# Output projection of a hybrid attention layer: eight products of quarters against Strassen's seven, and two ways to spread a row of scales

## The chip, the cores and the metric

One core of a Trainium2 chip. The metric is the device time in microseconds (us) of one execution; the kernel before has a median of 1061.15 us over three runs (1060.97 to 1061.85). The core has a matrix engine (TensorE, PE in the rows), VectorE (DVE), ScalarE (ACT), GpSimd (POOL) and the queue engine SP, which issues most DMAs. Each works through its own queue in order, and semaphores tie the queues together.

## The reference

One decoder layer in float32, 512 tokens, width 2048. The part that the change touches is the output projection and the norm behind it:

```
y = jnp.einsum('btm,md->btd', jnp.concatenate([o_a, o_b], axis=-1), w_out[l])
x = x + rmsnorm(y, norm_post_g[l])
```

`o_a` (8 heads x 128, differential attention) and `o_b` (8 heads x 128, sparse attention over latent keys) are each multiplied by a SiLU gate. The einsum is a product of 512x2048 and 2048x2048.

## The kernel before, in words

The kernel keeps activations transposed, as tiles of 128 features x 512 tokens. Precision comes from splitting: each float32 operand x becomes a high part (ScalarE's cast to float32r) and a low part (VectorE's x minus high), and a product is three matmuls, high x high, high x low and low x high.

**Weights.** `unit` (L55) lists every weight tile in the order of use. `load_to` (L90) loads a unit by a DMA on SP into one of two `wf` buffers, `split_to` (L104) splits it on ScalarE and VectorE (L124, L125) into one of three `wh` and three `wl` buffers, and `use` (L129) hands it to the matmuls and asks for the loads and splits of the units up to three or four ahead. Loads and splits get a priority up to 600 places earlier (`lead`, L86). The program is written in one order, and a scheduler that follows priorities and its own timeline sets the final order of each engine's queue.

**Spread.** `rstd` (L194) makes four columns of scales by a power on GpSimd. `spread` (L198) turns them into a row on all 128 partitions: GpSimd multiplies the identity by each column (L202, four times), and a matmul with a tile of ones sums it over the partitions (L203). It is called three times at the start (L217, L286, L306) and once in each head of group A (`head_a`, L524).

**Heads.** Eight heads of group A, then eight of group B (L585 on). `head_b` (L527) computes scores, softmax, transposes (L424) and values (L435); its transposed probabilities lie in tiles named pt0a, pt0b to pt3a, pt3b, and its result, times the gate, goes to `go[8 + h]` (L554). In head 7, before `head_b`, the finished gate tiles 0 to 14 are split (L590), and tile 15 at L593.

**Output projection (L598 to L669).** Four column blocks n of 512 columns. For n < 3, eight weight units (two contraction tiles each) are used in turn, and each serves four token blocks i: `part` (L605) issues 2 x 3 matmuls of 512 columns (L609 to L611). `done` (L613) squares a finished bank with its sum on ScalarE and multiplies it by the broadcast norm gain on VectorE (L617, one input in PSUM, one in SBUF). The last block, n = 3, keeps its eight units and goes token block by token block (L651 to L653), the last one in two halves of 256 columns, so that the residual (L633), the power (L661), the final scaling and addition (L668, L666) and the store (L669) of one block lie under the matmuls of the next.

Of the kernel before, what the change touches and what calls it, by code (L numbers as in the profile page):

```python
# [25 lines left out]
def hybrid_layer(tc, xT, xn, wck, wT, wik, wva, wuv, wo, gpre, gpost, sub, kvg, ikg, lq1, lk1, lq2, lk2, relb, oneh, out):  # L26
    nc = tc.nc
    from contextlib import ExitStack
    with ExitStack() as st:
# [50 lines left out]
        for n in range(4):  # L80
            for kp in range(8):
                unit(wo[n, kp], (2, 512))
        stage, ready, flags = {}, {}, {"begin": None}
# [5 lines left out]

        def load_to(n):  # L90
            while pos["load"] < min(n, len(units)):
# [4 lines left out]
                t = S.tile([128, 1024], F32, name=nm, bufs=bf)  # L96
                with tc.high_priority(lead()):
                    nc.sync.dma_start(t[:, :c], ap)
                stage[i] = t
                pos["load"] += 1  # L100

        last = [("qk", 4)] * 4 + [("v", 3)] * 3 + [("ck0", 1), ("ck1", 1)] + [("wh", 3), ("wl", 3)] * 3 + [("pt0a", 1)]

        def split_to(n):  # L104
            while pos["split"] < min(n, len(units)):
                i = pos["split"]
                load_to(i + 1)
                c = units[i][1][0] * units[i][1][1]
                t = stage.pop(i)
                names = [("wh", 3), ("wl", 3)]  # L110
                if i >= len(units) - 8:
                    names = [last.pop(0), last.pop(0)]
                w = []
                for nm, bf in names:
                    if nm == "pt0a":
                        w.append([S.tile([128, 512], F32R, name=x, bufs=1) for x in ("pt0a", "pt0b")])
                    else:
                        a = S.tile([128, 1024], F32R, name=nm, bufs=bf)
                        w.append([a[:, :512], a[:, 512:]] if units[i][1][1] == 512 else [a[:, :c]])
                m = c // len(w[0])  # L120
                with tc.high_priority(lead()):
                    for q in range(len(w[0])):
                        src = t[:, q * m:(q + 1) * m]
                        nc.scalar.copy(w[0][q], src)  # L124
                        nc.vector.tensor_tensor(w[1][q], src, w[0][q].bitcast(F32), op=OP.subtract)  # L125
                ready[i] = w
                pos["split"] += 1

        def use(ahead=3):  # L129
            i = pos["use"]  # L130
            pos["use"] += 1
            if ahead:
                load_to(i + ahead + 1)
                split_to(i + ahead)
            nk, n = units[i][1]
            w = ready.pop(i)
            per = nk // len(w[0])
            return [[w[a][k // per][:, (k % per) * n:(k % per + 1) * n] for k in range(nk)] for a in range(2)]
# [13 lines left out]
        ones = S.tile([128, 128], F32, name="ones")  # L152
        nc.gpsimd.memset(ones, 1.0)
# [422 lines left out]
        oh_, ol_ = [], []  # L576

        def split_o(m):
            a = S.tile([128, 512], F32R, name=f"hh{m}")
            b = S.tile([128, 512], F32R, name=f"hl{m}")  # L580
            split((a, b), go[m])
            oh_.append(a)
            ol_.append(b)

        for h in range(8):  # L585
# [3 lines left out]
            if h == 7:  # L589
                for m in range(15):  # L590
                    split_o(m)
# [6 lines left out]
        for n in range(4):  # L598
            gB = S.tile([128, 512], F32, name="strip", bufs=2)
            nc.gpsimd.dma_start(gB, bcast(gpost[n], 512))  # L600
            if n % 2 == 0:
                banks = [proj_bank(), proj_bank(), proj_bank(), lg_bank()]
            else:
                banks = [lg_bank(), tr_bank(), tr_bank(), av_bank()]
            def part(kp, i, wh, wl):  # L605
                ts = slice(i * 128, (i + 1) * 128)
                for k in range(2):
                    kk = 2 * kp + k
                    nc.tensor.matmul(banks[i], oh_[kk][:, ts], wh[k], start=(kk == 0), stop=False)  # L609
                    nc.tensor.matmul(banks[i], oh_[kk][:, ts], wl[k], start=False, stop=False)  # L610
                    nc.tensor.matmul(banks[i], ol_[kk][:, ts], wh[k], start=False, stop=(kk == 15))  # L611

            def done(i):  # L613
                junk = S.tile([128, 512], F32, name="a3")
                nc.scalar.activation(junk, banks[i], AF.Square, accum_out=ssy[:, i, n:n + 1])
                y = S.tile([128, 512], F32, name=f"go{i * 4 + n}")
                nc.vector.tensor_tensor(y, banks[i], gB, op=OP.mult)  # L617
                ys[i, n] = y

            if n < 3:  # L620
                for kp in range(8):
                    wh, wl = use()
                    for i in range(4):
                        part(kp, i, wh, wl)
                for i in range(4):
                    done(i)
                continue
            ws = []
            for i in range(4):
                xs = []  # L630
                for q in range(4):
                    xr = S.tile([128, 512], F32, name="e" if q < 2 else "tq", bufs=2)
                    nc.sync.dma_start(xr, xn[i * 128:(i + 1) * 128, q * 512:(q + 1) * 512])  # L633
                    xs.append(xr)
                y = S.tile([128, 512], F32, name=f"go{i * 4 + n}")
                ys[i, n] = y
                base = S.tile([128, 1], F32, name="base", bufs=2)
                nc.vector.tensor_reduce(base, ssy[:, i, :3], axis=mybir.AxisListType.X, op=OP.add)
                nc.vector.tensor_scalar(base, base, 1.0 / D, EPS, op0=OP.mult, op1=OP.add)
                ry = S.tile([128, 1], F32, name="ry", bufs=2)  # L640
                cuts = (0, 512) if i < 3 else (0, 256, 512)
                for a, b in zip(cuts, cuts[1:]):
                    o = (banks[i] if a == 0 else proj_bank())[:, a:b]
                    for kp in range(8):
                        if i == 0:
                            ws.append(use())
                        wh, wl = ws[kp]
                        for k in range(2):
                            kk = 2 * kp + k
                            ts = slice(i * 128, (i + 1) * 128)  # L650
                            nc.tensor.matmul(o, oh_[kk][:, ts], wh[k][:, a:b], start=(kk == 0), stop=False)  # L651
                            nc.tensor.matmul(o, oh_[kk][:, ts], wl[k][:, a:b], start=False, stop=False)
                            nc.tensor.matmul(o, ol_[kk][:, ts], wh[k][:, a:b], start=False,  # L653
                                             stop=(kk == 15))
                    junk = S.tile([128, 512], F32, name="a3")
                    sl = ssy[:, i, 3:4]
                    nc.scalar.activation(junk[:, :b - a], o, AF.Square, accum_out=sl)
                    nc.vector.scalar_tensor_tensor(ry if b == 512 else base, sl, 1.0 / D, base,
                                                   op0=OP.mult, op1=OP.add)
                    nc.vector.tensor_tensor(y[:, a:b], o, gB[:, a:b], op=OP.mult)  # L660
                nc.gpsimd.tensor_tensor(ry, ry, mhalf[:, 0:1], op=OP.pow)  # L661
                for q in range(4):
                    if i == 3 and q == 1:
                        t = S.tile([128, 512], F32, name="sq", bufs=1)
                        nc.scalar.activation(t, ys[i, q], AF.Copy, scale=ry)
                        nc.gpsimd.tensor_tensor(ys[i, q], t, xs[q], op=OP.add)  # L666
                    else:
                        nc.vector.scalar_tensor_tensor(ys[i, q], ys[i, q], ry, xs[q], op0=OP.mult, op1=OP.add)  # L668
                    nc.sync.dma_start(out[i * 128:(i + 1) * 128, q * 512:(q + 1) * 512], ys[i, q])  # L669
# [11 lines left out]
def _layout(inputs):  # L681
# [21 lines left out]
    wo = np.stack([tiles(f["w_out"].reshape(D, D)[:, 512 * n:512 * n + 512], 2) for n in range(4)])  # L703
# [33 lines left out]
```

## Time and profile before

| what | value |
|---|---|
| median of three runs | 1061.15 us |
| profiled execution, its own time | 1062.16 us |
| span of the profiled execution | 1060.1 us |
| TensorE busy | 1048.4 us (99%), 5403 matmuls |
| VectorE busy | 568.0 us (54%) |
| ScalarE busy | 420.9 us (40%) |
| GpSimd busy | 69.5 us (7%) |
| mean granted clock | 0.997 |

Times inside an execution count from the start of the span. The span ends with the last store; the profiled execution's own time is about 2 us longer than its span. A busy TensorE is not TensorE at its peak, since matmuls are pipelined and overlap in the rows.

### The profile page before, as it was taken

To read this page: it belongs to the slowest core of one execution; us is meant where nothing else is said; L and a number is where in the kernel's file an instruction comes from. 1 tells how busy PE (TensorE), PEld (TensorE's weight loads), DVE (VectorE), ACT (ScalarE), POOL (GpSimd) and SP (SyncE) were. 2 spreads that over 40 slices of the span, in tenths; PEclk is the share of its full clock that TensorE was granted. 3 is DMA by queue.
4 is the path that set the end of the run, shared out by engine and by line. 5 is a ranking of instruction groups with operands and counts; after the bars stand their busy time and mean duration, and the time that the engine had idled before them with its cause. 6 is when DMAs were issued, how large, how long until landed. Compare 5 with 4: busy or idle time off the path is not lost.

```text
span 1060.1 us, 13936 instructions
## 1 busy us (share of the span) xinstructions
PE 1048.4 (99%) x5403; PEld 898.0 (85%) x5403; DVE 568.0 (54%) x1144; ACT 420.9 (40%) x789; POOL 69.5 (7%) x102
## 2 busy tenths in 40 slices
PE   8999999999999999999999999999999999999996
PEld 6788988888889898899899888888888888888886
DVE  5344554469953564565465466654645484323353
ACT  6543343332223464464465365332323263322320
POOL 2112300000000002001101101100000000000001
PEclk9999999999999999999999999999999999999998
DMA  8623932232233322222222223222222233333445
GB/s 290 242 94 104 299 101 97 100 100 90 90 100 100 100 70 91 82 88 88 82 91 70 90 94 96 70 90 80 91 80 90 80 95 97 98 100 109 137 131 189
DMA packets 37265, 116.09 MB, mean 110 GB/s; under 512 B 4592, under 2 KB 4720, under 8 KB 37200
## 3 DMA queue, kind: packets, MB, share of 16 engines
q1 hardware_dynamic: 35280, 108.68, 31.4%
q0 software_dynamic: 1920, 6.53, 2.1%
q8 instruction: 42, 0.69, 0.3%
q14 instruction: 23, 0.19, 0.1%
HBM read 110.96 MB, written 9.48 MB: 114 GB/s over the span
## 4 chain that ended last, share of the span: by engine, by line
PE 97%; DMA 1%; SPq 1%; DVE 0%; issue 0%; ACT 0%; DVEq 0%; POOL 0%; ACTq 0%; POOLq 0%
PE pj L162 19%; PE pj L163 19%; PE pj L161 19%; PE pj L454 3%; PE pj L453 3%; PE pj L452 3%; PE lg L537 3%; PE av L435 3%; PE pj L609 2%; PE pj L611 2%; PE pj L610 2%; PE lg L259 2%; PE lg L261 2%; PE tr L424 2%; PE lg L611 1%; PE lg L610 1%
## 5 line engine op out<-in xcount | busy, mean ns | idle before, releaser
L163 PE MATMUL pj<-hh,wl 128*128 128x512 f32 (+2 forms) x912 | 353.2, 387 | 0.0
L162 PE MATMUL pj<-hl,wh 128*128 128x512 f32 (+2 forms) x912 | 350.9, 385 | 0.0
L161 PE MATMUL pj<-hh,wh 128*128 128x512 f32 (+2 forms) x912 | 350.8, 385 | 0.0
L124 ACT CAST wh<-wf 128x1024 fp32r<-128x1024 f32 (+2 forms) x181 | 164.8, 923 | 381.7 <-PE pj L162 174.3
L125 DVE TENSOR_TENSOR wl<-wf,wh 128x1024 fp32r<-128x1024 f32 (+2 forms) x181 | 192.0, 1072 | 207.9 <-ACT wh L124 207.7
L162 PEld LDWEIGHTS pj<-hl,wh 128*128 128x128 f32 (+1 forms) x912 | 170.7, 187 | 32.1 <-issue 1.6
L161 PEld LDWEIGHTS pj<-hh,wh 128*128 128x128 f32 (+1 forms) x912 | 170.8, 187 | 31.1 <-issue 1.4
L163 PEld LDWEIGHTS pj<-hh,wl 128*128 128x128 f32 (+1 forms) x912 | 170.7, 187 | 31.2 <-issue 1.2
L454 PE MATMUL pj<-wh,hl 128*128 128x256 f32 x256 | 74.4, 291 | 0.0
L452 PE MATMUL pj<-wh,hh 128*128 128x256 f32 x256 | 73.2, 286 | 0.0
L453 PE MATMUL pj<-wl,hh 128*128 128x256 f32 x256 | 72.7, 284 | 0.0
L265 DVE SCALAR_TENSOR_TENSOR tq<-pj,rB 128x512 f32<-128x512 f32 (+1 forms) x40 | 26.6, 664 | 65.6 <-PE pj L163 63.9
L452 PEld LDWEIGHTS pj<-wh,hh 128*128 128x128 f32 x256 | 48.8, 190 | 1.1 <-issue 0.7
L454 PEld LDWEIGHTS pj<-wh,hl 128*128 128x128 f32 x256 | 48.8, 190 | 0.8 <-issue 0.7
L453 PEld LDWEIGHTS pj<-wl,hh 128*128 128x128 f32 x256 | 48.8, 190 | 0.4
L537 PE MATMUL lg<-ck,qk 128*128 128x256 f32 (+3 forms) x192 | 38.4, 325 | 0.0
L610 PE MATMUL pj<-wl,hh 128*128 128x512 f32 x96 | 37.5, 390 | 0.0
L609 PE MATMUL pj<-wh,hh 128*128 128x512 f32 x96 | 37.3, 391 | 0.0
L611 PE MATMUL pj<-wh,hl 128*128 128x512 f32 x96 | 37.2, 390 | 0.0
L196 POOL TENSOR_TENSOR ro<-ro,mhalf 128x4 f32<-128x4 f32 x8 | 9.6, 1200 | 401.3 <-DVE ro L195 401.3
L537 PEld LDWEIGHTS lg<-ck,qk 128*128 128x128 f32 x192 | 32.0, 189 | 3.6 <-issue 0.2
L406 DVE SCALAR_TENSOR_TENSOR sc<-e,iw,sc 128x256 f32<-128x256 f32 (+2 forms) x45 | 27.7, 616 | 9.5 <-ACT e L402 7.7
(349 smaller groups left out, 1465.6 us busy)
## 6 DMA issues: line engine op xcount, KB each, us to landing
wf<-in_wT_dram SPq DMA_DIRECT2D x112, 512.0 KB, 3.5
wf<-in_wo_dram SPq DMA_DIRECT2D x32, 512.0 KB, 3.6
wf<-in_wva_dram SPq DMA_DIRECT2D x16, 512.0 KB, 3.5
table<-bd POOLq DMA_DIRECT2D x16, 320.0 KB, 10.8
go<-in_xT_dram SPq DMA_DIRECT2D x16, 256.0 KB, 6.1
v<-in_xn_dram SPq DMA_DIRECT2D x8, 512.0 KB, 5.1
strip<-table SPq DMA_DIRECT2D x16, 256.0 KB, 3.5
out_dram<-go SPq DMA_DIRECT2D x16, 256.0 KB, 3.6
```

The source lines that it names most:

```text
L124: nc.scalar.copy(w[0][q], src)
L125: nc.vector.tensor_tensor(w[1][q], src, w[0][q].bitcast(F32), op=OP.subtract)
L161: nc.tensor.matmul(ps, a, x, start=(k == 0), stop=False)
L162: nc.tensor.matmul(ps, a, y, start=False, stop=False)
L163: nc.tensor.matmul(ps, b, x, start=False, stop=(k == KT - 1))
L452: nc.tensor.matmul(o, hh[kk][:, ts], wh[k], start=(kk == 0 and i % 2 == 0), stop=False)
L453: nc.tensor.matmul(o, hh[kk][:, ts], wl[k], start=False, stop=False)
L454: nc.tensor.matmul(o, hl[kk][:, ts], wh[k], start=False, stop=(kk == 15 and i % 2 == 1))
L537: nc.tensor.matmul(bank[:, :w], q[u][:, x, i * 128:(i + 1) * 128], ck[u][:, y, :w], start=(n == 0), stop=(n == 5))
L609: nc.tensor.matmul(banks[i], oh_[kk][:, ts], wh[k], start=(kk == 0), stop=False)
L610: nc.tensor.matmul(banks[i], oh_[kk][:, ts], wl[k], start=False, stop=False)
L611: nc.tensor.matmul(banks[i], ol_[kk][:, ts], wh[k], start=False, stop=(kk == 15))
```

## The change

The projection is seen as a 2 x 2 matrix of quarters times a 2 x 2 matrix of quarters, twice (part p = 0, 1: 1024 output columns each). A's quarters: token halves (lo, up) x contraction halves (group A's tiles 0 to 7, group B's tiles 8 to 15); B's: contraction halves x 512 columns. Strassen's method in Winograd's form makes seven products in place of eight, with

- S1 = A21 + A22, S2 = S1 - A11, S3 = A11 - A21, S4 = A12 - S2;
- T1 = B12 - B11, T2 = B22 - T1, T3 = B22 - B12 (made as T2 - B11), T4 = B21 - T2.

S1 is made behind each head of group B (GpSimd, VectorE for the last), S2 to S4 on GpSimd behind head 7, the T tiles on GpSimd as part of the weight stream (`combine`). T1 loads two tiles into separate buffers, T2 to T4 work in place. The products' results are copied or added into result tiles by ScalarE, VectorE and GpSimd. The last product of part 1 goes token block by token block, the last block in halves, as before. In `use`, units of the projection are loaded up to five ahead. `spread` transposes the broadcast column of scales by TensorE.

The diff, cut to its core:

```
-        for n in range(4):
-            for kp in range(8):
-                unit(wo[n, kp], (2, 512))
+        plain = len(units)
+        for p in range(2):
+            for u in range(4):
+                unit(wo[p, 0, u], (2, 512))
+            for u in range(4):
+                unit(("t1", p, u), (2, 512))
+            for u in range(4):
+                for nm in ("t2", "b22", "t3"):
+                    unit((nm, p, u), (2, 512))
...
+        ring = [("wf", 2), ("wf", 2), ("ck1", 1)]
+        def raw(ap):
+            nm, bf = ring[0]
+            ring.append(ring.pop(0))
+            r = S.tile([128, 1024], F32, name=nm, bufs=bf)
+            nc.sync.dma_start(r, ap)
+            return [r[:, :512], r[:, 512:]], [r]
+        def combine(nm, p, u):
+            ks = (2 * u, 2 * u + 1)
+            if nm == "t1":
+                for q, k in enumerate(ks):
+                    T[k] = S.tile([128, 512], F32, name=f"hh{8 + k}")
+                    nc.sync.dma_start(T[k], wo[p, 1, u][:, q * 512:(q + 1) * 512])
+                    b = S.tile([128, 512], F32, name="e", bufs=2)
+                    nc.sync.dma_start(b, wo[p, 0, u][:, q * 512:(q + 1) * 512])
+                    nc.gpsimd.tensor_tensor(T[k], T[k], b, op=OP.subtract)
+                return [T[k] for k in ks]
...
+            if nm == "t3":
+                b, whole = raw(wo[p, 0, u])
+                for q, k in enumerate(ks):
+                    nc.gpsimd.tensor_tensor(b[q], T[k], b[q], op=OP.subtract)
+                return whole
...
+            for q, k in enumerate(ks):
+                nc.gpsimd.tensor_tensor(T[k], b[q], T[k], op=OP.subtract)
+            return [T[k] for k in ks]
...
-            dg = S.tile([128, 512], F32, name="dg")
             for i in range(4):
-                nc.gpsimd.tensor_scalar(dg[:, i * 128:(i + 1) * 128], ident, row[:, i:i + 1], None, op0=OP.mult)
-            nc.tensor.matmul(bank, ones, dg, start=True, stop=True)
+                nc.tensor.transpose(bank[:, i * 128:(i + 1) * 128], row[:, i:i + 1].to_broadcast([128, 128]), ident)
...
             head_b(h, q)
-        split_o(15)
+            eng = nc.gpsimd if h < 7 else nc.vector
+            eng.tensor_tensor(go[h][:, up], go[h][:, up], go[8 + h][:, up], op=OP.add)
...
+        for j in range(8):
+            t = S.tile([128, 512], F32, name="pt0b")
+            s3 = S.tile([128, 256], F32, name="pt2a")
+            nc.gpsimd.tensor_tensor(t[:, up], go[j][:, up], go[j][:, lo], op=OP.subtract)
+            nc.gpsimd.tensor_tensor(t[:, lo], go[8 + j][:, lo], t[:, up], op=OP.subtract)
+            nc.gpsimd.tensor_tensor(s3, go[8 + j][:, up], t[:, up], op=OP.subtract)
+            z = S.tile([128, 2, 512], F32R, name=zhome[j][0], bufs=zhome[j][1])
+            split((z[:, 0, :], z[:, 1, :]), t)
+            w = ws_[j]
+            split((w[:, 0, :], w[:, 1, :]), s3)
...
+        def product(banks, form, u):
+            w = use()
+            for i in range(2):
+                part(banks[i], form, i, u, w)
...
+            for u in range(4):
+                product(P6, "s2", u)
+                product(P3, "s4", u)
+                product(P7, "s3", u)
+            for i in range(2):
+                add(rc_[i], P6[i], ra[i])
+            for i in range(2):
+                add(rd[i], P3[i], rb_[i])
+                add(rd[i], rd[i], rc_[i], nc.gpsimd)
+                done(rd[i], i, n2, gBs[1])
+            for i in range(2):
+                add(rc_[i], P7[i], rc_[i])
+                add(rb_[i], rb_[i], rc_[i], nc.gpsimd)
+                done(rb_[i], 2 + i, n2, gBs[1])
```

`part` issues 2 x 3 matmuls per unit and token block, as before, over eight contraction tiles. `done` now squares and multiplies a result tile in SBUF.

## Rows read from the trace of the kernel before

**Rows 1.** The page, busy time: engine, busy us, share, instructions.
```profile
PE 1048.4 (99%) x5403; PEld 898.0 (85%) x5403; DVE 568.0 (54%) x1144; ACT 420.9 (40%) x789; POOL 69.5 (7%) x102
```
**Rows 2.** Windows over the projection: stretch, length, busy per engine, clock, DMA share, GB/s.
```profile
868.30:904.00 35.70, 35.70 (x177) 30.02 (x176) 18.36 (x42) 10.73 (x25) 0.55 (x1) 1.00 0.29 92
904.00:1052.00 148.00, 148.00 (x698) 124.07 (x696) 52.91 (x92) 39.26 (x83) 2.78 (x5) 1.00 0.41 128
1052.00:1060.10 8.10, 0.16 (x2) 0.00 (x0) 3.58 (x5) 1.20 (x3) 2.28 (x2) 0.63 0.34 129
```
**Rows 3.** Timeline, TensorE, the first and last of 33 matmuls: start, duration.
```profile
954.69 0.39 PE L610 MATMUL tr<-wl,hh 128*128 128x512 f32 x1
...
961.94 0.39 PE L609 MATMUL tr<-wh,hh 128*128 128x512 f32 x1
```
**Rows 4.** Chain in order of time: start, length; one spread, one group of transposes.
```profile
684.39 0.86 PE av L203 x2
...
835.46 0.33 PE tr L424 x3
```
**Rows 5.** Instructions by line and shape, and two splits in the timeline.
```profile
L124 ACT CAST wh<-wf 128x512 fp32r<-128x512 f32 x52 | 29.9, 618 | 71.6 <-PE av L611 30.1 <-PE lg L611 25.3 <-issue 10.2
L125 DVE TENSOR_TENSOR wl<-wf,wh 128x1024 fp32r<-128x1024 f32 x128 | 157.4, 1229 | 149.0 <-ACT wh L124 148.8
L125 DVE TENSOR_TENSOR wl<-wf,wh 128x512 fp32r<-128x512 f32 x52 | 33.8, 688 | 58.9 <-ACT wh L124 58.8
L241 DVE TENSOR_TENSOR pt2b<-tr,pt2a 128x256 fp32r<-128x256 f32 x16 | 6.7, 421 | 0.5
...
897.51 1.29 DVE L125 TENSOR_TENSOR wl<-wf,wh 128x512 fp32r<-128x512 f32 x2 [2.08 <-ACT wh L124]
```
**Rows 6.** VectorE beside GpSimd: single lines (min/median/max ns), and the timeline.
```profile
L666 POOL TENSOR_TENSOR go<-sq,e x1: 1736/1736/1736, 1054.4 to 1054.4; 128x512 f32<-128x512 f32 x1
L668 DVE SCALAR_TENSOR_TENSOR go<-go,ry,tq x8: 744/748/1752, 1021.7 to 1054.9; 128x512 f32<-128x512 f32 x8
L202 POOL TENSOR_SCALAR dg<-ident,ro x32: 592/605/1853, 403.1 to 679.4; 128x128 f32<-128x128 f32 x32
...
403.06 3.09 POOL L202 TENSOR_SCALAR dg<-ident,ro 128x128 f32<-128x128 f32 x4
403.77 1.33 DVE L125 TENSOR_TENSOR wl<-wf,wh 128x1024 fp32r<-128x1024 f32 x1 [1.72 <-ACT wh L124]
...
1054.25 2.42 DVE L668 SCALAR_TENSOR_TENSOR go<-go,ry,tq 128x512 f32<-128x512 f32 x2
1054.38 1.74 POOL L666 TENSOR_TENSOR go<-sq,e 128x512 f32<-128x512 f32 x1 [0.83 <-ACT sq L665]
```
**Rows 7.** Head 7: timeline, and the projection's matmuls between 868.3 and 904 us.
```profile
897.22 0.39 PE L435 MATMUL av<-pt0a,v 128*128 128x512 f32 x1
...
904.05 0.69 DVE L554 TENSOR_TENSOR go<-av,go 128x512 f32<-128x512 f32 x1 [4.71 <-PE av L435]
...
L610 PE MATMUL pj<-wl,hh 128*128 128x512 f32 x30 | 11.8, 393 | 0.0
...
L609 PE MATMUL lg<-wh,hh 128*128 128x512 f32 x10 | 4.0, 400 | 0.0
```
**Rows 8.** Timeline of the end: the gain on 256 columns.
```profile
1052.78 0.42 DVE L660 TENSOR_TENSOR go<-pj,strip 128x256 f32<-128x256 f32 x1
```
**Rows 9.** Timeline, SP's queue: one issue of a weight DMA.
```profile
865.06 0.33 SPq L98 DMA_DIRECT2D wf<-in_wo_dram  x1
```
**Rows 10.** The page, GB/s in 40 slices of the span.
```profile
GB/s 290 242 94 104 299 101 97 100 100 90 90 100 100 100 70 91 82 88 88 82 91 70 90 94 96 70 90 80 91 80 90 80 95 97 98 100 109 137 131 189
```
**Rows 11.** DMA issues: count, KB each, median us to landing.
```profile
wf<-in_wo_dram SPq DMA_DIRECT2D x32, 512.0 KB, 3.6
...
go<-in_xT_dram SPq DMA_DIRECT2D x16, 256.0 KB, 6.1
...
e<-in_xn_dram SPq DMA_DIRECT2D x8, 256.0 KB, 3.4
```

More of the change, by code (lines that the diff above doesn't have):

```diff
@@ L108, in split_to @@
                 c = units[i][1][0] * units[i][1][1]
-                t = stage.pop(i)
+                src = stage.pop(i)
                 names = [("wh", 3), ("wl", 3)]
-                if i >= len(units) - 8:
+                if i >= len(units) - 4:
                     names = [last.pop(0), last.pop(0)]
[L113 to L120, printed above, removed]
+                w = [S.tile([128, 1024], F32R, name=nm, bufs=bf)[:, :c] for nm, bf in names]
+                m = c // len(src)
                 with tc.high_priority(lead()):
[L122 to L125, printed above, removed]
+                    for q, t in enumerate(src):
+                        x, y = (z[:, q * m:(q + 1) * m] for z in w)
+                        nc.scalar.copy(x, t)
+                        nc.vector.tensor_tensor(y, t, x.bitcast(F32), op=OP.subtract)
                 ready[i] = w
@@ L132, in use @@
             if ahead:
-                load_to(i + ahead + 1)
+                load_to(i + ahead + (3 if i >= plain else 1))
                 split_to(i + ahead)
             nk, n = units[i][1]
-            w = ready.pop(i)
-            per = nk // len(w[0])
-            return [[w[a][k // per][:, (k % per) * n:(k % per + 1) * n] for k in range(nk)] for a in range(2)]
+            return [[w[:, k * n:(k + 1) * n] for k in range(nk)] for w in ready.pop(i)]
         warm = S.tile([128, 1], F32, name="warm")
@@ L151, in hybrid_layer @@
         nc.vector.memset(onec, 1.0)
-        ones = S.tile([128, 128], F32, name="ones")
-        nc.gpsimd.memset(ones, 1.0)
         ident = S.tile([128, 128], F32, name="ident")
@@ L574, in hybrid_layer, with split_x @@
             pass
[L576 to L583, printed above, removed]
+        lo, up = slice(0, 256), slice(256, 512)
+        xs_, F = [], {}
+        def split_x(j, cs):
+            if j == len(xs_):
+                xs_.append([S.tile([128, 512], F32R, name=f"{nm}{j}") for nm in ("hh", "hl")])
+            a, b = xs_[j]
+            split((a[:, cs], b[:, cs]), go[j][:, cs])
         for h in range(8):
@@ new lines, in hybrid_layer, with two @@
+        for j in range(8):
+            y = S.tile([128, 512], F32R, name=f"hl{8 + j}")
+            small = S.tile([128, 512], F32R, name=f"go{7 + j}" if j else "a3")
+            split((y, small), go[8 + j])
+            F["a12", j], F["a22", j] = ([y[:, cs], small[:, cs]] for cs in (lo, up))
+            F["a11", j], F["s1", j] = ([t[:, cs] for t in xs_[j]] for cs in (lo, up))
+        ring8 = [proj_bank, proj_bank, proj_bank, lg_bank, lg_bank, tr_bank, tr_bank, av_bank]
+        def two():
+            r = [ring8[0](), ring8[1]()]
+            ring8.extend(ring8[:2])
+            del ring8[:2]
+            return r
@@ new lines, in part @@
+        def part(bank, form, i, u, w, cs=slice(0, 512)):
+            wh, wl = w
+            ts = slice(i * 128, (i + 1) * 128)
+            for k in range(2):
+                kk = 2 * u + k
+                a, b = F[form, kk]
+                nc.tensor.matmul(bank, a[:, ts], wh[k][:, cs], start=(kk == 0), stop=False)
+                nc.tensor.matmul(bank, a[:, ts], wl[k][:, cs], start=False, stop=False)
+                nc.tensor.matmul(bank, b[:, ts], wh[k][:, cs], start=False, stop=(kk == 7))
@@ new lines, in more, with final @@
+        def more(dst, i, n, base):
+            nc.vector.scalar_tensor_tensor(dst, ssy[:, i, n:n + 1], 1.0 / D, base, op0=OP.mult, op1=OP.add)
+        def final(i, ry, xs):
+            nc.gpsimd.tensor_tensor(ry, ry, mhalf[:, 0:1], op=OP.pow)
+            for q in range(4):
+                if i == 1 and q == 1:
+                    t = S.tile([128, 512], F32, name="pt0b", bufs=1)
+                    nc.scalar.activation(t, ys[i, q], AF.Copy, scale=ry)
+                    nc.gpsimd.tensor_tensor(ys[i, q], t, xs[q], op=OP.add)
+                else:
+                    nc.vector.scalar_tensor_tensor(ys[i, q], ys[i, q], ry, xs[q], op0=OP.mult, op1=OP.add)
+                nc.sync.dma_start(out[i * 128:(i + 1) * 128, q * 512:(q + 1) * 512], ys[i, q])
@@ L702, in _layout @@
     wuv = uv.transpose(0, 3, 2, 1, 4).reshape(4, 128, 512)
-    wo = np.stack([tiles(f["w_out"].reshape(D, D)[:, 512 * n:512 * n + 512], 2) for n in range(4)])
+    wout = f["w_out"].reshape(2, 1024, 2, 2, 512).transpose(2, 0, 3, 1, 4)
+    wo = wout.reshape(2, 4, 4, 2, 128, 512).transpose(0, 1, 2, 4, 3, 5).reshape(2, 4, 4, 128, 1024)
     return {
```

209 lines of the change are left out of this document (133 added, 76 removed).

## The prediction

> **What bounds the kernel now.** I read the busy shares first. TensorE is busy for 99% of the span, VectorE for 54%, ScalarE for 40%, GpSimd for 7% [rows 1]. The reader is to see that the three others have room as a mean over the span. Then I cut the end of the span into stretches: TensorE is busy without a gap from 868 us, where the first matmul of the output projection starts, to 1052 us, at a granted clock of 1.00, which is the 2.4 GHz level. In the 148 us behind the last head VectorE works for 53 us, ScalarE for 39 and GpSimd for 2.8 [rows 2]. So a matmul that is taken away is a gain, so long as what the other engines must do in its place fits beside the rest.
>
> In the list of instructions a matmul shows 390 ns, but that is its passage through the pipeline; the price is the distance between starts. From 954.69 to 961.94 us stand 33 matmuls of 512 columns: 7.25 / 32 = 0.2266 us each [rows 3].
>
> **What it takes away.** The projection has 4 column blocks x 16 contraction tiles x 4 token blocks x 3 = 768 such matmuls (some of them in halves). After the change it has 2 parts x 7 products x 8 contraction tiles x 2 token blocks x 3 = 672. The 96 that go are worth 96 x 0.2266 = **21.8 us**, all on the path. 76.1 us of TensorE remain per part.
>
> The spread of a row of scales is now two passes of the ones matmul, 0.86 us on the chain; three transposes of 128 columns take 0.33 us there [rows 4], so four take 0.44. There are 11 spreads (three at the start, eight in the heads of group A): 11 x 0.42 = **4.6 us**. The trace has no transpose of a broadcast column; the bounds are 0 and 4.6 us, and I take 4.6, because it loads and streams as many columns as the transposes shown. GpSimd's four multiplies per spread (605 ns each) go too, but TensorE never stood idle for them, so I count nothing for that. Together the gain is 26.4 us.
>
> **What it adds.** Each weight tile now serves 12 matmuls (2.7 us), not 24. 56 units are split in place of 32. On VectorE a split is a subtraction with both inputs in SBUF: 1.23 us for 1024 columns, 0.69 for 512, 0.42 for 256; two of 512 in a row take 1.29 [rows 5], so 0.09 of each is overlap, and I count 1.14, 0.60 and 0.33. ScalarE's part (0.62 us per half [rows 5], 56 x 1.24 = 69 us) has room in some 160 us, also with 4 copies and 8 squares of the same length per part. The new part is GpSimd: per part 32 subtractions of 512 columns for T1 to T4 and 4 additions of results; in part 0 also 24 of 256 columns for S2, S3 and S4.
>
> The one GpSimd tensor_tensor of 512 columns in the trace is the key row. It shows 1736 ns, and the VectorE instruction beside it 1752 ns, where its like take 748 [rows 6]. In order of time: VectorE's second operation ends at about 1055.00; GpSimd's, started at 1054.38, ends at 1056.12; VectorE's third, started at about 1054.9, ends at 1056.67. So GpSimd waited for the second, then took 1.12 us, and held the third back by 1752 - 748 = 1.00 us. Both VectorE operations have two inputs in SBUF. GpSimd's multiplies in the heads show it from the other side: 605 ns as median, 1853 at most, 1.25 us more, as long as a VectorE split of 1024 [rows 6]. I read from this that such operations of the two engines take turns. The Trainium skill ("SBUF — State Buffer", section "Who interferes with whom") gives it as a rule: a VectorE instruction with two SBUF inputs and a GpSimd instruction that reads SBUF share a read interface, whichever starts first has it for its whole length, and the other is blocked. The trace agrees (1752 against 748 ns). By this rule the sum is the forecast below, without it the first rival.
>
> So VectorE's two-input work and GpSimd's work are to be added. GpSimd's 512 columns count 1.00; its 256 columns have no row: I take 0.50 by proportion, with 0.25 and the 0.605 of a whole GpSimd multiply as bounds.
>
> **Part 0.** S2 to S4 go through buffers that head 7 uses (pt0b and pt2a), so they can't begin before its value matmuls have read pt0b, at 897.2 us [rows 7], 892.6 after the gain of the spreads. From there the pair has to do:
> - S2 to S4: 8 x (3 x 0.50 + 0.60 + 0.33) = 19.4;
> - splitting A12 and A22: 8 x 0.60 = 4.8;
> - T2 and T3: 16 subtractions, two of them ahead of this point: 14 x 1.00 = 14.0;
> - splits of T2, B22, T3: 4 x (1.20 + 1.14 + 1.14) = 13.9, and one of T1, 1.2;
> - T4: 8.0, and the splits of T4 and B21: 4 x 2.34 = 9.4;
> - four GpSimd additions and the gains on their results (now two SBUF inputs): 4.0 + 2.4.
>
> The sum is 77.1, which ends at 969.7; the last unit's 12 matmuls end at 972.4. The last matmul ends 0.16 us behind 1052.00 [rows 2], so by TensorE alone part 0 would end at 1052.2 - 26.4 - 76.1 = 949.7. **Part 0 is late by 22.7 us.**
>
> In this stretch two waits cost nothing more, as this cover lies over them. Before, 120 projection matmuls filled the gaps of the last heads up to 904 us [rows 7]; now only P1 and three quarters of P5 (84) are ready then, so up to 36 x 0.2266 = 8.2 us of gap appear. And S1 of tile 7 needs head 7's product with its gate (904.05, 0.69 us), an addition of 256, a copy and a split of 256: some 2.3 us. If the turns cost nothing, these 10.5 us come to light.
>
> **Part 1.** P1 and P5: 4 x 1.14 + 4 x 3.20 + 2.4 of part 0's results = 19.8 beside 21.8 of TensorE. P6, P3, P7: 4 x (4.00 + 3.48) = 29.9 beside 32.6. P4: 12.8 + 4.0 + 2.4 = 19.2 beside 10.9, of which 4.7 fit ahead: 3.6 late. P2: 4 x 1.20 for B21, eight final operations at 0.66 and two gains, 11.3 beside 10.9. **About 4 us late.** Both engines work through their queues in order, and at 92% use they can't always take turns without a gap: between 0 and 25 us over both parts (a quarter of some 100 us); I take 6, near the lower end, because GpSimd's results are what VectorE splits next, so the turns partly follow by themselves.
>
> **The end.** Now the last matmul is followed by a square, the mean, the power and four operations. An addition of 256 columns from PSUM comes ahead, priced like the gain of 256 columns [rows 8], 0.42, and a handover of some 0.1: +0.5 us.
>
> **Other queues.** SP issues 68 weight DMAs in place of 32, at 0.33 us each [rows 9], 22 us of issue in 160: hidden. The traffic rises from 32 to 48 times 512 KB, 16.8 to 25.2 MB, about 160 GB/s, under the 299 that a slice shows [rows 10]. T1 loads two tiles per subtraction, one of them through a ring of two buffers: behind that wait on SP stand the next units' loads. With 3.4 us to landing [rows 11], 1.1 of GpSimd and 0.5 of handover (an estimate: the wait from 1054.38 to 1055.00, 0.62 [rows 6], now and then), two tiles take 5.0 us, four units 20 us, which P1 and P5 (21.8) just cover. GpSimd's queue also issues the broadcasts of the gain; each waits until the last reader of its buffer is through, and T subtractions stand behind it, with 20 us of P1 and P5 as cover. Copies of P1 and P5 into the old gate tiles wait until S2 has read them, no later than S2 itself.
>
> **Sum.** -26.4 + 22.7 + 4 + 6 + 0.5 = +6.8 us. The profiled execution took 1062.16 us (span 1060.1), 1.0 above the median of 1061.15; against the median it is **1068 us**. Its own range is 1055 (256-column operations at 0.25, no gaps) to 1087 (gaps of 25).
>
> **Rivals.** *TensorE stays the bound* (0.32). One event of 1752 ns carries the price of a turn, and four GpSimd multiplies in a row (3.09 us) stretched a split of 1024 only to 1.33 us [rows 6]: blocks may be far shorter than the instruction. At 0.65 us per GpSimd operation of 512 columns part 0's sum falls to 64 us and its lateness to the 10 us of the two waits; from there down TensorE decides. Then -26.4 + 0.5 and those waits, 0 to 10.5: 1035 to 1046, middle 1041. *Late tiles and a lower clock* (0.12). Under load 256 KB took 6.1 us to land, not 3.4 [rows 11]; T1 then takes 4 x 7.7 = 31 us beside 21.8, 9 us late in part 1. If TensorE's new waits bring the 1.2 GHz level, each matmul there costs 0.2266 us more; a tenth of part 1's 336 is 8 us. Against it: the granted clock falls only behind the last matmul so far [rows 2]. 1068 + 17 = 1085. That the matmuls don't go is excluded by the count.
>
> **How the numbers follow.** The forecast has 0.56, the rivals 0.32 and 0.12. A measurement can tell about 0.2%, 2 us. Of the forecast's case 0.04 lies below 1059, 0.06 within 2 us, 0.46 above. Faster: 0.32 + 0.04 = 0.36; same 0.06; slower 0.46 + 0.12 = 0.58. The range reaches to the middle of the first rival and past the second: 1040 to 1090.
>
> **What would show it.** Right: projection matmuls still 0.227 us apart but in bursts; GpSimd's 512-column subtractions well over 1.12 us as a mean, splits over 1.23; TensorE waiting for VectorE's splits and these for GpSimd, most in part 0's P6, P3, P7; spreads at 0.44 us. Wrong: TensorE gapless from 868 us with splits at 1.2 us (first rival), or waits on DMAs and a clock under 1.00 (second).

## The result, and the profile after

| | before | after |
|---|---|---|
| median | 1061.24 us (4 runs) | 1086.12 us (4 runs, 1085.14 to 1087.13) |
| ratio, 95% interval | | 1.0232 (1.022 to 1.0245) |
| span of the profiled execution | 1060.1 us | 1084.7 us |
| mean granted clock | 0.997 | 0.987 |

The changed kernel is 24.9 us slower. The forecast was 6.9 us slower (1068): the sign was right and the time lies inside the range of 1040 to 1090, but the size is not right, and the range of the forecast's own case, up to 1087, only just holds it (its lower end adds up to 1056, not 1055).

The page of the changed kernel, busy time, answers to [rows 1]:

```profile
PE 1036.8 (96%) x5305; PEld 882.9 (81%) x5305; DVE 676.5 (62%) x1207; ACT 457.1 (42%) x834; POOL 183.7 (17%) x160
```

TensorE is busy for 11.6 us less. VectorE is busy for 108.5 us more and GpSimd for 114.2 more; how much of that is waiting, which the page counts as busy, is the question below.

The windows of the changed kernel (columns as in [rows 2]), cut where P6 of part 0 takes over (the last six matmuls of P5 follow among its first, until 911 us), at the end of part 0, and at the last matmul:

```profile
864.10:903.80 39.70, 35.10 (x165) 28.25 (x163) 28.55 (x44) 16.66 (x36) 25.83 (x21) 0.96 0.45 152
903.80:986.40 82.60, 63.83 (x242) 47.43 (x242) 72.92 (x66) 34.58 (x59) 62.98 (x47) 0.94 0.36 113
986.40:1072.80 86.40, 80.39 (x361) 64.77 (x359) 77.38 (x86) 36.78 (x66) 56.09 (x34) 0.98 0.50 167
1072.80:1084.70 11.90, 0.00 (x0) 0.00 (x0) 7.72 (x14) 1.41 (x5) 3.20 (x3) 0.68 0.46 177
```

The reader is to see the second line: TensorE works in 64 of 82.6 us, VectorE in 73 and GpSimd in 63. The bound has moved. By TensorE alone part 0 would end at 949.7 us (worked out in the prediction); it ends at 986.4, 36.7 us late. Part 1 takes 86.4 where TensorE needs 76.1, 10.3 late. The end behind the last matmul takes 11.9 in place of 7.9, 4.0 more. With the 26.4 us that the prediction takes away, -26.4 + 36.7 + 10.3 + 4.0 = +24.6, which is what the span grew by.

The instructions of the changed kernel from 850 us on, by line and shape (busy us, mean ns | idle before), answer to [rows 5]:

```profile
L186 DVE TENSOR_TENSOR wl<-hh,wh 128x512 fp32r<-128x512 f32 x48 | 55.7, 1199 | 5.0 <-ACT wh L185 4.7
L186 DVE TENSOR_TENSOR wl<-wf,wh 128x1024 fp32r<-128x1024 f32 x19 | 32.0, 1689 | 3.4 <-ACT wh L185 3.3
L186 DVE TENSOR_TENSOR wl<-ck,wh 128x1024 fp32r<-128x1024 f32 x9 | 15.8, 1760 | 3.0 <-ACT wh L185 3.0
...
L149 POOL TENSOR_TENSOR hh<-wf,hh 128x512 f32<-128x512 f32 x16 | 27.3, 1726 | 4.3 <-DVE wl L186 4.3
```

A split of 512 columns takes 1199 ns where it took 688, one of 1024 takes 1689 to 1760 where it took 1229. TensorE's waits name the same lines (waits of the changed kernel, 880 to 1073 us: who <- releaser, us in total, times, longest):

```profile
PEld pj L702 <- DVE wl L186: 10.5, 7, 3.8
...
PEld lg L702 <- DVE wl L186: 9.1, 5, 3.6
...
PE pj L702 <- DVE wl L186: 7.6, 5, 3.4
```

TensorE waits for low halves (VectorE's L186), and ScalarE, the step before, waits 10.6 us for GpSimd's T tiles. That is the picture which the prediction said would show it right. But a wait shows who was late, not why, so the turns were tested.

### The profile page after: what moved, and what is told of

Same layout as the page of the kernel before. It is cut to its first block, busy times and chain, and to the rows that moved or that the text cites. A ratio compares the mean times of both kernels' runs of the same rounds, so it can differ in the third digit from the quotient of the medians.

```text
span 1084.7 us, 14079 instructions
## 1 busy us (share of the span) xinstructions
PE 1036.8 (96%) x5305; PEld 882.9 (81%) x5305; DVE 676.5 (62%) x1207; ACT 457.1 (42%) x834; POOL 183.7 (17%) x160
## 4 chain that ended last, share of the span: by engine, by line
PE 76%; DVE 9%; DMA 5%; issue 4%; POOL 3%; ACT 1%; SPq 1%; DVEq 0%; POOLq 0%; ACTq 0%
PE pj L220 18%; PE pj L219 18%; PE pj L218 18%; DVE wl L186 5%; PE pj L510 3%; PE pj L509 3%; PE pj L508 3%; PE lg L593 2%; PE av L491 2%; PE lg L315 2%; PE tr L480 2%; POOL hh L149 2%; PE lg L317 1%; DMA e<-in_wo_dram 1%; DMA wf<-in_wT_dram 1%
## 5 line engine op out<-in xcount | busy, mean ns | idle before, releaser
L185 ACT CAST wh<-wf 128x1024 fp32r<-128x1024 f32 (+1 forms) x152 | 157.3, 1035 | 351.2 <-PE pj L219 187.2
L186 DVE TENSOR_TENSOR wl<-wf,wh 128x1024 fp32r<-128x1024 f32 (+1 forms) x152 | 192.2, 1265 | 153.0 <-ACT wh L185 152.6
L219 PEld LDWEIGHTS pj<-hl,wh 128*128 128x128 f32 (+1 forms) x912 | 170.7, 187 | 30.1
L186 DVE TENSOR_TENSOR wl<-hh,wh 128x512 fp32r<-128x512 f32 x48 | 55.7, 1199 | 5.0 <-ACT wh L185 4.7
L185 ACT CAST wh<-hh 128x512 fp32r<-128x512 f32 x48 | 27.3, 617 | 25.3 <-POOL hh L149 10.6
L480 PE MATMUL tr<-ident,a 128*128 128x128 f32 x160 | 30.3, 275 | 4.6 <-DVE a L605 4.6
L654 POOL TENSOR_TENSOR go<-go,go 128x256 f32<-128x256 f32 x7 | 6.3, 896 | 161.2 <-DVE go L610 161.2
```

Of the source, the lines that this page charges most:

```text
L185: nc.scalar.copy(x, t)
L186: nc.vector.tensor_tensor(y, t, x.bitcast(F32), op=OP.subtract)
L219: nc.tensor.matmul(ps, a, y, start=False, stop=False)
L480: nc.tensor.transpose(bank[:, (i - j) * 128:(i - j + 1) * 128], a[i][:, j * 128:(j + 1) * 128], ident)
```

## Experiments

The theory: VectorE's operations with two SBUF inputs and GpSimd's operations exclude each other, and the length of the turns sets the projection. The rivals: GpSimd is simply too slow for 500 ns matmul work; the two engines have too much work even without turns; loads, or one buffer of the load ring, set the pace. In the table, the last column is the difference of the ratios to the kernel before, times 1061 us.

| run | what differs | median us | ratio (95%) | against the changed kernel, us |
|---|---|---|---|---|
| e1_spread | before, with the new spread alone | 1058.53 | 0.9972 (0.996 to 0.9983) | -27.6 |
| e2_memset | GpSimd as busy, but writes only | 1055.54 | 0.9948 (0.993 to 0.9967) | -30.1 |
| e3_onecol | GpSimd's operations one column | 1051.33 | 0.9905 (0.9887 to 0.9923) | -34.7 |
| e4_vector | all of GpSimd's new work on VectorE | 1068.91 | 1.0075 (1.0061 to 1.0088) | -16.7 |
| e5_ring | another buffer for the third raw tile | 1083.9 | 1.0213 (1.0198 to 1.0229) | -2.0 |
| e6_vecring | e4 and e5 | 1063.12 | 1.0027 (1.0013 to 1.0041) | -21.8 |
| e7_tail | e6, end reordered | 1063.74 | 1.0025 (1.0014 to 1.0035) | -22.0 |
| e8_svec | only S2 to S4 on VectorE | 1081.31 | 1.019 (1.0173 to 1.0207) | -4.5 |
| e9_floor | e3 and e5 | 1043.89 | 0.9836 (0.9816 to 0.9856) | -42.0 |
| e10_nofinal | e6 without eight last operations | 1060.68 | 0.9987 (0.9978 to 0.9997) | -26.0 |
| e11_afternofinal | the changed kernel without them | 1083.49 | 1.0202 (1.0187 to 1.0217) | -3.2 |

### Are the turns the cause? (e2, e3)

e2 keeps GpSimd about as long at work, but takes away its reads, all but one column (the values are left out):

```diff
+def short(dst, x, y, op=OP.subtract):
+    n = dst.shape[1]
+    nc.gpsimd.tensor_tensor(dst[:, :1], x[:, :1], y[:, :1], op=op)
+    for _ in range(2):
+        nc.gpsimd.memset(dst[:, 1:], 0.5)
...
-    nc.gpsimd.tensor_tensor(T[k], b[q], T[k], op=OP.subtract)
+    short(T[k], b[q], T[k])
```

> The changed kernel, but each large GpSimd operation (T1 to T4, S2 to S4, the additions of results) is cut to its first column, followed by two memsets of the other columns, which read nothing. GpSimd stays occupied about as long and in the same place of every chain (the values are left out). If the time is lost because VectorE's two-input operations and GpSimd's reads take turns, VectorE's splits fall back to 0.69 us per 512 columns and 1.23 per 1024, and the time to about 1040 (1035 to 1048). If it is lost because GpSimd is slow at 1.3 us and stands in the chain from load to split, the time stays above 1075.

Instructions of e2 from 850 us on:

```profile
L192 DVE TENSOR_TENSOR wl<-hh,wh 128x512 fp32r<-128x512 f32 x48 | 31.1, 684 | 13.8 <-ACT wh L191 13.8
...
L121 POOL MEMSET hh<- 128x511 f32 x104 | 51.9, 525 | 4.1 <-DVE wl L192 1.8 <-DMA hh<-in_wo_dram 1.7
```

The splits are back at 684 ns [rows 5: 688] beside a GpSimd that is busy for 154.6 us of the run, and the time falls by 30. So it is GpSimd's reading of SBUF that stretches VectorE, not its being busy. The rival of a slow GpSimd falls: one column (0.2 us) and two fills (0.52 each) make T about as late as a subtraction that nothing holds up (1.28 us, below). The rival of too much work without turns falls with it, since VectorE has the same instructions beside it. The page of e2 also answers how much of VectorE's busy time was waiting:

```profile
PE 1031.0 (98%) x5305; PEld 881.4 (83%) x5305; DVE 615.7 (58%) x1207; ACT 456.7 (43%) x834; POOL 154.6 (15%) x352
```

The same 1207 instructions take 60.8 us less than in the changed kernel (676.5). But 1055.5 is well above the 1048 at the upper end of what was expected. e3 leaves the fills out (all but one on the tiles of S2 to S4), which shows what GpSimd's own length costs:

```diff
-    for _ in range(2):
-        nc.gpsimd.memset(dst[:, 1:], 0.5)
+    if fill:
+        nc.gpsimd.memset(dst[:, 1:], 0.5)
```

> As the one with memsets, but without the two memsets (one only, of 256 columns, where S2 to S4 need a tile that is written): GpSimd's work is nearly gone. Both theories expect a time at or under that of the kernel with memsets; the difference between the two is what GpSimd's length in the chains costs without turns. By turns: 0 to 3 us. By a slow GpSimd in the chain: 30 us or more. The time itself shows what seven products cost when only the splits are left: 1035 to 1045.

4.2 us by the medians, a little over the 0 to 3 expected (e2's own three runs lie 5.1 us apart), and far from the 30 of a slow GpSimd. What holds e3 above its expectation stands in its windows, columns as before:

```profile
875.00:880.00 5.00, 1.86 (x11) 1.30 (x9) 2.27 (x7) 1.63 (x4) 1.10 (x4) 1.00 0.64 206
880.00:885.00 5.00, 1.43 (x5) 0.80 (x6) 1.03 (x3) 1.86 (x4) 0.00 (x0) 0.57 0.49 157
885.00:890.00 5.00, 4.96 (x12) 3.38 (x12) 4.26 (x6) 2.44 (x5) 1.03 (x4) 0.50 0.52 192
```

TensorE is idle for 6.7 of 10 us in the last head, and then it is granted half its clock (0.50, the 1.2 GHz level) and gets through 12 matmuls in 5 us. That gap is new, and it led to e5 and e9.

### The gap in head 7 (e5, e9)

The timeline of SP's queue in the changed kernel shows where the gap starts:

```profile
871.79 6.34 SPq L126 DMA_DIRECT2D e<-in_wo_dram  x4
878.23 0.38 SPq L114 DMA_DIRECT2D ck<-in_wo_dram  x1
```

The third raw tile of the ring lies in ck1, which head 7's scores read until about 877 us, and its load stands on SP behind the loads of T1. The prediction spoke of SP's loads of T1, but of this buffer it said nothing. e5 puts that tile, the first time round, into a buffer that is free:

```diff
-ring = [("wf", 2), ("wf", 2), ("ck1", 1)]
+ring = [("wf", 2), ("wf", 2), ("qk", 4)]
...
-    nm, bf = ring[0]
-    ring.append(ring.pop(0))
+    nm, bf = ring.pop(0)
+    ring.append(("ck1", 1) if nm == "qk" else (nm, bf))
```

> The changed kernel, but the projection's third raw weight tile goes into a buffer of the q tiles that is free before head 7, in place of ck1, which head 7's scores read to the end. That takes away the late load of P1's third unit and so most of TensorE's gap in head 7 (in the run with one column, 6.7 us idle and then some 5 us lost at a clock under 1.00, between 876 and 895 us). If the turns of VectorE and GpSimd set part 0's end anyway (my prediction's view that the gap is covered), the time stays within 3 us of the changed kernel's 1086. If the gap adds to them, it falls by 7 to 12 us.

> The run with one column of GpSimd's work (1051.3 us) and the free buffer for the third tile: no turns and no late load. What is left is the seven products, the new spread and a longer end. If these three causes are all there is, 1061.2 - 26.1 + 4 = 1039 to 1042; if it stays above 1047, another wait in the transition is still unnamed.

The same edit is worth 2.0 us in the changed kernel and 7.4 us on e3. This is the cover that the prediction named for the filler of head 7 (up to 8.2 us), measured from both sides: while VectorE and GpSimd are what is late, an idle TensorE early in the projection costs little. The loads as a whole are no rival either: e5 and e9 load the same tiles into the same buffers and are 40 us apart (1083.9 and 1043.9). e9 ends 2 to 5 us above what was expected. Its windows over the place of the gap:

```profile
875.00:880.00 5.00, 5.00 (x27) 4.25 (x26) 1.53 (x5) 1.72 (x4) 1.31 (x5) 1.00 0.95 303
880.00:885.00 5.00, 5.00 (x25) 4.10 (x24) 4.01 (x10) 3.47 (x8) 2.03 (x4) 1.00 0.19 67
```

The gap is gone. What holds the other few microseconds was not traced to one wait.

### The same work on one engine (e4, e6, e8)

If turns are the cause, VectorE should be better off doing GpSimd's work itself, as a subtraction of 512 columns costs it 0.60 us in a row and a GpSimd turn costs it more. These kernels compute everything.

```diff
-nc.gpsimd.tensor_tensor(T[k], b[q], T[k], op=OP.subtract)
+nc.vector.tensor_tensor(T[k], b[q], T[k], op=OP.subtract)
...
-add(rd[i], rd[i], rc_[i], nc.gpsimd)
+add(rd[i], rd[i], rc_[i])
```

> The changed kernel with T1 to T4, S2 to S4 and the additions of results on VectorE in place of GpSimd; the output is complete. By turns a 512-column operation costs the pair 0.60 us on VectorE and 1.1 to 1.3 on GpSimd, so moving everything to the busier engine shortens the sum: part 0 from some 92 us to 69, and the time to about 1053 (1045 to 1062). If the two engines worked beside each other, VectorE would get some 40 us more work and the time would rise above 1090.

The page of e4:

```profile
PE 1032.9 (97%) x5305; PEld 880.9 (82%) x5305; DVE 664.2 (62%) x1303; ACT 456.7 (43%) x834; POOL 42.1 (4%) x64
```

VectorE carries 96 instructions more than in the changed kernel and shows 12.3 us less busy time (664.2 against 676.5), and the kernel is 17 us faster. This is the plainest reading of the case, and it agrees with e2: a part of the 676.5 us was waiting for GpSimd. The rival by which VectorE has no room for this (over 1090) falls. The time is not at the 1045 to 1062 expected: in the window that part 0 had in the changed kernel (in e4 it holds part 0, to about 976 us, and the first 10 us of part 1) TensorE is still idle for 9 of 82.6 us, where VectorE alone now works for 75.3 (e4, columns as before):

```profile
903.80:986.40 82.60, 73.45 (x291) 54.94 (x290) 75.34 (x125) 38.37 (x68) 1.11 (x2) 0.96 0.42 144
```

e8 moves the 24 operations for S2 to S4 alone, e6 adds e5's buffer to e4.

> The changed kernel with S2 to S4 alone on VectorE (T1 to T4 and the additions stay on GpSimd). By turns, 24 operations of 256 columns fall from some 0.6 to 0.33 us, about 7 us of the 17 that all the moves together gave: 1077 to 1081. If S2 to S4 made most of part 0's delay, since they bunch behind head 7, it comes down to 1072 or under.

> All the combinations on VectorE (1068.9 us) and the free buffer for the third tile. VectorE alone is less behind than the pair was, so less of the gap is covered: 1060 to 1065 if VectorE still sets most of part 0, 1057 if the gap of some 11 us counts in full.

S2 to S4 make 4.5 of the 16.7 us, the T tiles and the additions the other 12.2; e8's 1081.3 lies at the upper end of the 1077 to 1081 expected. e6 gains 5.1 us over e4: with the turns gone the gap of head 7 has lost part of its cover here too. With e7 below, which does not differ from it beyond the noise, it is the fastest complete kernel with seven products, and still 0.1 to 0.4% slower than the one before.

### The spread alone (e1)

```diff
-dg = S.tile([128, 512], F32, name="dg")
 for i in range(4):
-    nc.gpsimd.tensor_scalar(dg[:, i * 128:(i + 1) * 128], ident, row[:, i:i + 1], None, op0=OP.mult)
-nc.tensor.matmul(bank, ones, dg, start=True, stop=True)
+    nc.tensor.transpose(bank[:, i * 128:(i + 1) * 128], row[:, i:i + 1].to_broadcast([128, 128]), ident)
```

> The kernel before, with only the new spread (four transposes of the broadcast column in place of GpSimd's multiplies and the matmul of ones). If the spread is worth what the two traces show between their last spreads (685.3 against 681.0 us), this kernel takes 4.3 us less than before: 1057. If it was the new order of the queues that gave those 4.3 us, it stays within 1 us of 1061.

It gains 2.6 us by the medians, 3.3 by the spans (1056.8 against 1060.1), against 4.6 predicted. The operation that follows a spread (L525 before, L521 in e1), with its first and last start, in the one kernel and in the other:

```profile
L525 DVE TENSOR_TENSOR go<-go,av x8: 680/686/689, 408.9 to 685.3; 128x512 f32<-128x512 f32 x8
```

```profile
L521 DVE TENSOR_TENSOR go<-go,av x8: 676/686/689, 405.5 to 679.6; 128x512 f32<-128x512 f32 x8
```

From the first to the last, seven spreads later, e1 gains 5.7 - 3.4 = 2.3 us: 0.33 each, not 0.42. Eleven make 3.6. e1 is 5.7 us ahead at the last spread and 3.3 at the last matmul; where it loses the rest was not found. e1 is the fastest complete version of all: 0.2 to 0.4% faster than the kernel before.

### The end (e7, e10, e11)

The timeline of VectorE at the end of the changed kernel (start, us; the last matmul starts at 1072.51 and ends at 1072.78):

```profile
1070.27 0.74 DVE L745 SCALAR_TENSOR_TENSOR hh<-hh,ry,pt0a 128x512 f32<-128x512 f32 x1
1070.94 0.68 DVE L714 TENSOR_TENSOR hh<-pj,hh 128x512 f32<-128x512 f32 x1
...
1074.36 1.41 DVE L745 SCALAR_TENSOR_TENSOR go<-go,ry,hh 128x512 f32<-128x512 f32 x2
1075.69 1.41 DVE L745 SCALAR_TENSOR_TENSOR hh<-hh,ry,hh 128x512 f32<-128x512 f32 x2
1077.01 0.15 DVE L735 SCALAR_TENSOR_TENSOR ry<-ssy,base 128x1 f32<-128x1 f32 x1
```

The last operations of token blocks 2 and 3 (L745) stand ahead of block 0's addition (L714 at 1070.94), and block 0's ahead of block 1's input to the power (L735). e7, on e6, puts in the program those of blocks 2 and 3 behind the additions, and block 0's behind block 1's power.

> The kernel with all combinations on VectorE and the free buffer (1063.1 us), but the final operations of token blocks 2 and 3 stand behind the additions of blocks 0 and 1 in the program, and those of block 0 behind the power of block 1. If the end is 4 us longer than before because VectorE does 16 final operations late and in the wrong order, this gives back 1 to 3 us: 1060 to 1062. If VectorE's sum of work at the end sets it, whatever the order, the change is under 1 us.

No change, but the timeline shows that the order was not tested. VectorE's queue at the end of e7 (L747 is the last operation, L714 an addition, L735 block 1's input to the power):

```profile
1049.17 0.75 DVE L747 SCALAR_TENSOR_TENSOR hh<-hh,ry,pt0a 128x512 f32<-128x512 f32 x1
...
1050.50 0.42 DVE L714 TENSOR_TENSOR hh<-pj,hh 128x256 f32<-128x256 f32 x1
...
1053.38 1.41 DVE L747 SCALAR_TENSOR_TENSOR hh<-hh,ry,hh 128x512 f32<-128x512 f32 x2
1054.70 0.15 DVE L735 SCALAR_TENSOR_TENSOR ry<-ssy,base 128x1 f32<-128x1 f32 x1
```

This is e6's order (there 1048.84, 1050.11, 1053.36 and 1054.68 us): the scheduler set the queue as before, whatever the order in the program. What another order would give stays open. e10 (on e6) and e11 (on the changed kernel) leave eight of these operations out:

```diff
-                else:
+                elif i < 2:
                     nc.vector.scalar_tensor_tensor(ys[i, q], ys[i, q], ry, xs[q], op0=OP.mult, op1=OP.add)
```

> The kernel of e6_vecring, with the last scaling and residual addition of token blocks 2 and 3 left out (eight VectorE operations of 512 columns; these blocks are stored unscaled, the stores stay). What stretches the end is in question: e6's last store ends 13.6 us behind its last matmul, the kernel before's 7.9. Theory: it is VectorE's queue. These eight operations (0.67 us apart, 5.3 us) stand ahead of the additions of blocks 0 and 1 that the seventh product now needs; without them block 0 is done before the last matmul, and behind it stand one addition of 256 columns (0.42), a square, the power (about 0.9), four last operations (3.1) and a store (3.6): an end of about 9 us, 1058 to 1059.5 us. Rival: the end is the chain of the added operations and the stores themselves, whatever stands ahead: an end of over 12.5 us, 1062 to 1064. As the last operations also keep VectorE from nothing else, no third case is expected; between 1060 and 1062 both would have a share.

> The changed kernel, with the same eight operations left out (blocks 2 and 3 are stored unscaled). Its last store ends 11.9 us behind its last matmul, 4.0 more than before. Theory of VectorE's queue: the end falls to about 8.5 to 9 us and the time to 1082.5 to 1083.5; the last matmul stays where it is, within 1 us of 1072.8. Rival, the chain of added operations and stores: within 1 us of 1086.1.

The last matmul of e11 starts here, in its timeline:

```profile
1072.97 0.28 PE L703 MATMUL lg<-v,go 128*128 128x256 f32 x1
```

It ends at 1073.25 and the span at 1082.5: an end of 9.3 us in place of 11.9. In e10, where the last matmul ends at 1049.94 and the span at 1059.8, it is 9.9 in place of e6's 13.7. By the ratios the time falls by 3.2 and 4.2 us (by the medians 2.6 and 2.4). So most of the longer end is VectorE's queue: 2.6 of the 4.0 us go with these eight operations; that the other 1.4 are the added operations and the rest of that queue is argued, not shown. e10's 1060.7 lies between the two cases of its expectation; its end of 9.9 us is nearer to the theory's 9 than to the rival's 12.5.

## Why the prediction was right in sign and wrong in size

**What it takes away: right, with one term too large.** The 672 matmuls need their time: P1 and P5 of part 1 take 22.6 us (986.4 to 1009.0) for 96 x 0.2266 = 21.8. The spreads measured 0.33 each for 0.42, 3.6 us in all (2.6 to 3.3 by e1) for 4.6.

**The turns: mechanism right, the sum for part 0 too small.** The step that failed is this term of the sum: "Part 0 is late by 22.7 us". It measured 36.7, 14.0 more, and the 6 us that I allowed for gaps did not cover that. The trace gives three sizes for the 14.0.

The first is the price of a GpSimd operation, "GpSimd's 512 columns count 1.00; its 256 columns ... 0.50", taken from a single pair of instructions [rows 6]. Now there are many. Where nothing stands beside it, a GpSimd subtraction of 512 columns takes 1.28 us, the least of these (min/median/max ns in the changed kernel), and one of 256 columns on this line 0.79:

```profile
L149 POOL TENSOR_TENSOR hh<-wf,hh x16: 1280/1736/2280, 886.2 to 1022.8; 128x512 f32<-128x512 f32 x16
```

```profile
L669 POOL TENSOR_TENSOR pt0b<-go x8: 789/1120/1717, 895.8 to 949.6; 128x256 f32<-128x256 f32 x8
```

The steadiest turns of the changed kernel's timeline give the price of a whole turn:

```profile
995.51 12.71 DVE L186 TENSOR_TENSOR wl<-hh,wh 128x512 fp32r<-128x512 f32 x10
...
999.61 3.47 POOL L134 TENSOR_TENSOR wf<-hh,wf 128x512 f32<-128x512 f32 x2
1003.04 3.43 POOL L149 TENSOR_TENSOR hh<-wf,hh 128x512 f32<-128x512 f32 x2
```

Two GpSimd operations take 3.43 us with as many splits between them: one turn of each is 1.71 us, of which the split has 0.60 and GpSimd 1.11. A turn thus hides 0.17 of the 1.28, and by the same allowance 256 columns count about 0.6 (an estimate from the 0.79). At 1.11 and 0.6 in place of 1.00 and 0.50 part 0's sum (24 of 256 columns, 26 of 512 with the additions) grows by 24 x 0.1 + 26 x 0.11 = 5.3 us.

The second is the last line of that sum, "the last unit's 12 matmuls". The last split for which TensorE stood still in part 0 ended at 978.4 us (969.7 in the sum):

```profile
978.49 0.50 PE L702 MATMUL lg<-wl,hl 128*128 128x512 f32 x1 [2.03 <-DVE wl L186]
```

From there TensorE is busy to 986.4 without a gap. It had 35 matmuls left at that point, not 12: 7.9 us in place of 2.7, 5.2 more.

The third, some 3.5 us, is work that "part 0" of my sum did not hold, and idle time. T1 of part 1 was fetched and subtracted before part 0 ended: four of its subtractions (from 963.35 us on) stand ahead of 978.4, 4.4 us at 1.11, against two of T2 and T3 more than I counted that were done early. And GpSimd, working its queue in order, stood still at some places, as here, for a tile's load:

```profile
920.48 3.00 POOL L149 TENSOR_TENSOR hh<-ck,hh 128x512 f32<-128x512 f32 x2 [3.09 <-DMA ck<-in_wo_dram]
```

Turns that miss each other, which the 6 us stood for, were not where part 0's time went. Between 892.4 and 978.4 us the timelines hold 28 GpSimd operations of 512 columns and 24 of 256, and on VectorE, with two inputs in SBUF, 11 of 1024, 37 of 512 and 11 of 256. At 1.11, 0.6, 1.14, 0.60 and 0.33 they add up to 83.8 of the 86.0 us. So one sum for both engines holds closely here, and what I put into it was too little.

**Part 1: right by chance.** 10.3 us late, where 4 and the 6 of gaps were forecast. But it falls elsewhere: P6, P3, P7 take 39.6 us (1009.0 to 1048.6) for 32.6 of matmuls, 7.0 late where I had them covered, and P4, where I had 3.6, is 2.0 late.

**The end: wrong.** +0.5 was the addition alone. I counted the operations behind the last matmul and not those queued ahead of them on VectorE, which the new order of token blocks (2 and 3 first) brings together there: +4.0, of which e11 takes 2.6 back. With part 0's 14.0, part 1's 6.3 and 3.5 here, less the 6 of gaps, this makes the 17.8 us between +6.8 and +24.6.

**Two waits at nothing: right for the first**, the gap in head 7, as e5 (2.0 us) against e9 (7.4 us) shows, though I had not seen that the ck1 buffer opens it. The second, S1 of tile 7, no run takes by itself.

**The rivals.** "TensorE stays the bound" (0.32) asked for splits at 1.2 us for 1024 columns; they take 1.7. e9 shows what it would have been worth: 1043.9, not 1041. "Late tiles and a lower clock" (0.12): T1's loads did not make P1 and P5 of part 1 late (22.6 for 21.8), so that half is wrong. The clock did fall, but behind TensorE's waits for VectorE, in the window here of the changed kernel, where TensorE was idle for 4.4 of 10 us:

```profile
910.00:920.00 10.00, 5.60 (x17) 3.75 (x16) 9.25 (x8) 6.05 (x10) 7.31 (x7) 0.84 0.19 55
```

I take the lower clock for an effect of the waits; no run separates the two. It was not quite free: on the chain that ended last seven matmuls between 917.4 and 920.0 us start 0.43 us apart in place of 0.23, about 1.2 us.

## What to carry to other kernels

Where VectorE's instructions take both inputs from SBUF and GpSimd's read SBUF, as here, the time of both belongs into one sum: a "free" GpSimd is then about half as fast a VectorE that makes the real one wait (1.11 us for 0.60 here), and the page's busy share of either holds that waiting. So cost moved work against the pair, try it on the one engine first (e4 was 17 us faster than the split), and count what stands ahead in a queue at the end, not only what is added behind the last matmul. A change of two parts is worth taking apart: the small one (e1, -2.6 us) was the gain, the large one the loss.

## What was not expected of the hardware

VectorE's operation with one tensor input in SBUF also waited. In head 7 the scaling of the probabilities, a tensor-by-column multiplication (VectorE and GpSimd in the changed kernel's timeline):

```profile
872.87 0.95 DVE L605 TENSOR_SCALAR a<-a,sm 128x128 f32<-128x128 f32 x1
...
881.00 1.08 DVE L605 TENSOR_SCALAR a<-a,sm 128x384 f32<-128x384 f32 x1
```

```profile
872.45 1.28 POOL L127 TENSOR_TENSOR hh<-hh,e 128x512 f32<-128x512 f32 x1 [0.68 <-PE lg L593]
...
880.60 1.26 POOL L127 TENSOR_TENSOR hh<-hh,e 128x512 f32<-128x512 f32 x1 [0.88 <-issue]
```

128 columns take 0.95 us, where in the kernel before not even 512 columns took more than 0.489 (the largest of that line's 32). Both end just behind the GpSimd subtraction beside them, by 0.09 and 0.22 us (873.82 against 873.73, 882.08 against 881.86), so they waited, it seems, for its end and then took little time of their own. They are the only two of that line's 32 that started beside a GpSimd operation. The Trainium skill ("SBUF — State Buffer", "Who interferes with whom") says that such one-input operations, when they run in a mode that uses both ports, contend with GpSimd for the whole instruction. The trace agrees in the time (0.95 against at most 0.489 us); which mode the instruction ran in no run here shows. The same section has a GpSimd instruction that only writes SBUF leave a two-input one of VectorE alone, and e2 agrees: 684 ns beside 525 ns fills. VectorE's additions with one input in PSUM and one in SBUF did not wait: the one at 963.71 us took 0.68 us in the middle of a GpSimd subtraction (963.35 to 964.93).
